# A Transformer-layer kernel on one core: second-half weight blocks of the MLP in a ring of tiles kept to the end, right operands of its last two products and the last rows' sums made among its middle products

## The chip, the core and the metric

The kernel runs on one core of one Trainium2 chip. The metric is the device time of one execution in microseconds (us); lower is better. Times of the program as a whole are given as the median of the runs, a profile is of one execution. TensorE is the matrix engine (PE in the rows), VectorE (DVE) and ScalarE (ACT) do the elementwise work, GpSimd (POOL) does a little, and SyncE (SP) issues the DMAs.

## The reference

One layer with a latent stream of 1024 tokens and 1024 channels, and a context of 256 tokens. All is float32. A mixer (adaLN, a projection, spatial gating, a two-way chunkwise mLSTM and an output projection) is followed by an MLP with 4096 hidden channels; each adds to the stream through a LayerNorm:

```python
def channel_mlp(h, w1, b1, w2, b2):
    return jnp.square(jax.nn.relu(h @ w1 + b1)) @ w2 + b2

def deepnorm_update(x, y, gate, g, b):
    return layer_norm(ALPHA * x + gate * y, g, b)

# in reference(), for the one layer:
y_l = mixer_output(u_l, v_l, hb_l, o_l, w_s[l], b_s[l], ln_v_g[l], ln_v_b[l], hn_g[l], w_out[l])
x_new = deepnorm_update(x, y_l, g1, ln1_g[l], ln1_b[l])
x_new = deepnorm_update(x_new, channel_mlp(modulate(x_new, sh2, sc2), w1[l], b1[l], w2[l], b2[l]),
                        g2, ln2_g[l], ln2_b[l])
```

## The kernel before

The mixer takes the time up to about 490 us; the MLP takes the rest. Each of the MLP's two matrix products is cut in two by two blocks and computed with seven block products in place of eight, so their operands are blocks, or sums and differences of blocks. A float32 operand is split into a high part (a cast on ScalarE) and a low part (a subtraction on VectorE), and each block product is three passes on TensorE: high by low, high by high, low by high (`mmk`, L983).

**Phase 1** (h times w1, then the squared ReLU) goes over 16 groups of 128 hidden channels per half, in batches of 4, 3, 3, 3 and 3 (`BATCHES`). For each group there are two weight blocks of 128x1024: X (`load_x`, L1075) and Y (`load_y`, L1079). `prep_w1(p, g)` makes the right operand wc_p_g of product p for group g: of X alone for p = 2 and 1, and for p = 5 the difference w1z of X and Y (kept for p = 7) and the sum of the two halves of Y (L1098, L1100), for p = 6 and 3 further differences of X (L1103, L1106), and then cast and low part (L1112, L1113). The left operands are h itself for p = 2 and 1, and sums of its parts for the others: `t_add` forms them (T2 for p = 6 stands in a tile of its own, L1149), `t_split` makes the parts T50h, T50l, T51h and so on (L1164, L1165). The first four groups are special: `first(2, g)` and `first(1, g)` (L1307) run while the last token tiles of h are still being made (`h2_half`), with casts of X made earlier (x0h, x0l). Then the loop over `steps` runs: for the first batch the products 5, 6, 3, 7 and 4, four groups each (12 matmuls of 128x512 a group), and then the other batches with all seven. Ahead of each step `prep_to` prepares operands LA = 5 steps ahead, `load_to` issues loads LD = 6 steps further ahead, and `tplan` says before which step which T sum and T part is made.

**Phase 2** (the hidden blocks times w2) goes over the products 1, 2, 6, 5, 3, 7, 4 and in each over 8 steps c. A step takes a block a of the left operand (loaded from DRAM, where phase 1 left it) and a right operand of w2 (`p2_load`, L1190), splits both (`p2_prep`, L1209: the parts of a go to pb, those of the right operand to wh and wl, L1206 and L1207), and multiplies for four token tiles (`p2_mm`, 24 matmuls). The right operands are T1 = b11, for p = 2 b21, for p = 6 T2 = b22 minus T1, for p = 5 T1 again (by then b12 minus b11), for p = 3 b22, for p = 7 b22 minus b12 (L1234), for p = 4 b21 minus T2 (L1239); for the last two, b12 and b21 are loaded once more as b12b and b21b in the steps of 7 and 4 themselves. The loop prepares LA2 = 3 steps ahead and asks for loads LD2 = 2 steps further ahead. After a product's last step the sums in PSUM are evacuated: after p = 3 c12 (L1471, L1472) and after p = 7 c22 (L1476, in a tile of the pool whose name shows as pm).

**The end.** The rows of the first four token tiles are finished among the steps of products 7 and 4 (`half1`, L1436). Of product 4 the steps c = 4 to 7 are done token tile by token tile, and each of the last four tiles t = 0 to 3 is finished behind its matmuls: residual (L1422), the gated sum r (L1488, L1491), `finish` (L1424) with the row sum (L1428), mean, variance (ScalarE), power (GpSimd) and the two steps of the last LayerNorm (L1430, L1431), and the output store. The last tile goes in two column halves of 256 and takes its statistics with BN_STATS (L1495 to L1511).

**Tiles and order.** Phase 1 and 2 share a ring of 38 slots of 4 KB per partition, `uslots`: `ualloc` takes the slot that has been free longest, `ufree` puts one back. 9 of the slots (ur) exist from before the first groups, 29 (ul) only when the mixer's pools (wpool, rawp and others) are closed behind `first(1, 3)`. rawp is a pool of four turning buffers for raw weight blocks of the mixer. Each engine runs its instructions in program order, with semaphores for what it needs of others; every DMA of the program is issued by SP, in program order too.

```python
    for g in range(3):
        load_x(g)
    ...
    rst.close()
    wst.close()
    u_open(ctx, USLOTS[1], "ul")
    ...
    for g in range(n0):
        load_y(g)
    load_x(3)
```

## Time and profile before

| what | value |
|---|---|
| median of three runs | 1126.34 us (1125.4 to 1127.55) |
| the profiled execution | 1127.33 us |
| its span, first to last instruction | 1125.4 us |
| busy share of the span: PE / PEld / DVE / ACT / POOL | 97% / 80% / 68% / 46% / 5% |
| DMA traffic | 208.08 MB, mean 185 GB/s |
| the chain of work that ended last, by engine | PE 89%, DVE 4%, DMA 3%, ACT 2% |

A span is the time between the first and the last instruction in the records; the execution's own time is 1.9 us longer. The granted clock of TensorE is given for a stretch as a share of its full 2.4 GHz; 1.00 is all of it, 0.50 is its lower level of 1.2 GHz, and what lies between is a stretch with both. A start time plus a duration can lie behind the start of the next row of the same engine, since instructions overlap a little.

### The profile page before, as it was taken

Reading aid. Unit: us, or ns where it says so; the run is one execution under the profiler, and the core shown is the slowest. Engines: PE = TensorE matmul, PEld = TensorE weight load, DVE = VectorE, ACT = ScalarE, POOL = GpSimd, SP = SyncE. Lnnn points to the kernel's source line nnn. Section 1 sums busy time; section 2 is a strip of 40 time slices with the busy share of each in tenths; the row PEclk is TensorE's granted clock in tenths of the full one; section 3 lists DMA queues with packets and bytes.
Section 4 is the critical chain, followed back from the end, with each engine's and each line's share of the span. In section 5 each row is a group of like instructions: output and inputs, shape, how many; then the busy total and the mean of one; then the engine's idle time right before and its main releaser. Section 6 shows DMA issues by size and latency. Waiting matters only on the chain.

```text
span 1125.4 us, 14624 instructions
## 1 busy us (share of the span) xinstructions
PE 1094.6 (97%) x5271; PEld 899.9 (80%) x5271; DVE 761.5 (68%) x1363; ACT 517.6 (46%) x821; POOL 53.6 (5%) x81
## 2 busy tenths in 40 slices
PE   8999999899999999997999999999999999999996
PEld 6899788777777888885888888888888888887875
DVE  4793666677775367659974747474667555468997
ACT  3585543321121236567755555556534334434341
POOL 0010000000101011110000000000000000001101
PEclk9999999999999999998999999999999999999999
DMA  8782579776453773233454435355997334356911
GB/s 319 259 280 95 169 255 293 236 204 175 127 155 113 260 238 129 85 112 112 151 195 127 175 123 183 112 197 201 321 413 271 113 90 152 96 168 235 326 57 75
DMA packets 92416, 208.08 MB, mean 185 GB/s; under 512 B 10037, under 2 KB 31413, under 8 KB 92089
## 3 DMA queue, kind: packets, MB, share of 16 engines
q1 hardware_dynamic: 92344, 207.16, 55.0%
q8 instruction: 41, 0.67, 0.2%
q14 instruction: 31, 0.25, 0.1%
HBM read 155.91 MB, written 51.21 MB: 184 GB/s over the span
## 4 chain that ended last, share of the span: by engine, by line
PE 89%; DVE 4%; DMA 3%; ACT 2%; issue 1%; POOL 1%; SPq 0%; DVEq 0%; ACTq 0%; POOLq 0%
PE A L986 29%; PE B L986 23%; PE wo L209 3%; PE wo L207 3%; PE wo L208 3%; PE n L736 2%; PE n L735 2%; PE pa L270 2%; PE v L207 2%; PE vg L209 1%; PE vg L208 1%; PE vg L207 1%; PE u L207 1%; PE v L209 1%; PE v L208 1%; PE u L209 1%
## 5 line engine op out<-in xcount | busy, mean ns | idle before, releaser
L986 PE MATMUL A<-wh,pb 128*128 128x512 f32 (+1 forms) x528 | 158.6, 383 | 0.0
L986 PE MATMUL B<-wh,pb 128*128 128x512 f32 x384 | 118.7, 390 | 0.0
L986 PEld LDWEIGHTS A<-wh,pb 128*128 128x128 f32 x528 | 98.0, 188 | 19.8
L986 PE MATMUL A<-wl,pb 128*128 128x512 f32 (+1 forms) x264 | 101.7, 385 | 3.2 <-DVE nmu_n L874 1.5
L986 PEld LDWEIGHTS B<-wh,pb 128*128 128x128 f32 x384 | 72.1, 188 | 15.6
L986 PE MATMUL B<-wl,pb 128*128 128x512 f32 x192 | 74.9, 390 | 0.0
L1206 ACT CAST pb<-a_S 128x1024 fp32r<-128x1024 f32 x32 | 33.7, 1053 | 75.1 <-PE B L986 43.8
L880 POOL TENSOR_TENSOR rs_n<-ve_n,mhalf 128x1 f32<-128x1 f32 x23 | 29.4, 1279 | 720.2 <-DVE ve_n L878 681.4
L1113 DVE TENSOR_TENSOR wc<-w1x,wc 128x512 fp32r<-128x512 f32 x56 | 38.3, 692 | 35.9 <-ACT wc L1112 35.9
L1207 DVE TENSOR_TENSOR wl<-b,wh 128x1024 fp32r<-128x1024 f32 x40 | 48.7, 1222 | 19.9 <-ACT wh L1206 6.9
L986 PEld LDWEIGHTS A<-wl,pb 128*128 128x128 f32 x264 | 49.6, 188 | 14.5 <-DVE nmu_n L874 1.7
L1207 DVE TENSOR_TENSOR pb<-a_S,pb 128x1024 fp32r<-128x1024 f32 x32 | 39.1, 1223 | 31.7 <-ACT pb L1206 31.5
L1206 ACT CAST wh<-b 128x1024 fp32r<-128x1024 f32 x40 | 42.0, 1051 | 33.4 <-DVE pb L1207 16.0
L207 PE MATMUL wo<-lo_W,yh 128*128 128x512 f32 x128 | 52.0, 406 | 0.0
L209 PE MATMUL wo<-hi_W,yl 128*128 128x512 f32 x128 | 50.7, 396 | 0.0
L208 PE MATMUL wo<-hi_W,yh 128*128 128x512 f32 x128 | 50.5, 394 | 0.0
L207 PE MATMUL vg<-lo_VG,Hhi 128*128 128x264 f32 x160 | 45.9, 287 | 0.0
L209 PE MATMUL vg<-hi_VG,Hlo 128*128 128x264 f32 x160 | 45.4, 284 | 0.5 <-DVE Hlo L198 0.5
L707 ACT ACTIVATE nmb<-nmb 128x512 f32<-128x512 f32 x16 | 10.1, 633 | 76.8 <-DVE nmb L706 46.6
L208 PE MATMUL vg<-hi_VG,Hhi 128*128 128x264 f32 x160 | 45.3, 284 | 0.0
L1112 ACT CAST wc<-w1x 128x512 fp32r<-128x512 f32 x56 | 34.4, 619 | 22.4 <-PE A L986 10.6
L1206 ACT CAST pb<-a_A 128x1024 fp32r<-128x1024 f32 x24 | 25.3, 1054 | 41.4 <-PE A L986 20.3
(412 smaller groups left out, 2773.7 us busy)
## 6 DMA issues: line engine op xcount, KB each, us to landing
ad<-in_wada SPq DMA_DIRECT2D x32, 512.0 KB, 6.1
b<-in_w SPq DMA_DIRECT2D x32, 512.0 KB, 5.2
a_S<-d_S SPq DMA_DIRECT2D x32, 512.0 KB, 4.1
d_S<-hF SPq DMA_DIRECT2D x50, 256.0 KB, 2.2
a_A<-d_A SPq DMA_DIRECT2D x24, 512.0 KB, 5.0
d_A<-hF SPq DMA_DIRECT2D x36, 256.0 KB, 2.0
wa<-in_wada SPq DMA_DIRECT2D x16, 512.0 KB, 6.2
w1x<-in_w SPq DMA_DIRECT2D x16, 512.0 KB, 3.6
```

What stands on the lines that cost most here:

```text
L207: T.matmul(o, ahi, blo, start=start, stop=False)
L208: T.matmul(o, ahi, bhi, start=False, stop=False)
L209: T.matmul(o, alo, bhi, start=False, stop=stop)
L270: T.matmul(pa[:, 0:256], s32[:, k, :], rv[k // 4][:, k % 4, :], start=(k == 0), stop=(k == KT - 1))
L735: T.matmul(pn[:, hh, :], nmb[d][:, h, :], vc[:, h, :], start=True, stop=False)
L736: T.matmul(pn[:, hh, :], wib[o : o + 64, h, :], st[o : o + 64, h, :], start=False, stop=True)
L880: G.tensor_tensor(rs, ve, mhalf[:, :1], op=ALU.pow)
L986: T.matmul(o, a, b, start=start and i == 0, stop=stop and i == 2, skip_group_check=more)
L1112: S.copy(t[:, 0:512], src)
L1113: V.tensor_tensor(t[:, 512:1024], src, t[:, 0:512].bitcast(F32), ALU.subtract)
L1206: S.copy(hi, src)
L1207: V.tensor_tensor(lo, src, hi.bitcast(F32), ALU.subtract)
```

## The change

**Loads of the first Y blocks.** rawp is opened ahead of wpool and kept to the end; its buffers become four named tiles raw0 to raw3, used in turn (`raw_tile`). Behind the casts of the first four X blocks, `load_y(0)` to `load_y(3)` load the Y blocks into these four tiles, and the tiles then stay in the ring as slots. The ring has 38 slots as before: 10 early ones (ur), 24 late ones (ul) and these four; `UL_ORDER` gives the order in which the late ones come into it. Two X blocks are loaded early now, where three were, and the other two behind the closing of the pools. `prep_w1(5, 0)` is called ahead of the last `h2_half`, and in the loop `load_to` and `prep_to` now stand ahead of the step's T sums and parts.

**Right operands of the last two products.** b12b is loaded in the steps of p = 3, and b22 minus b12 is formed in place there (L1252); b21b is loaded in the steps c < 4 of p = 3 and c >= 4 of p = 5, and T2 is replaced there by b21 minus T2 (L1256). The steps of p = 7 and p = 4 only split.

**Last rows.** `second(t)` takes, for each of the last four token tiles, the residual and the half of r that is complete after p = 7, with its row sum (L1444, L1445); the four are done one behind each of the steps c = 0 to 3 of p = 4. `finish` then sums only the other half (L1455) and adds the two sums (L1456). For the last tile the matmuls of both column halves come first, then all of VectorE's work on them.

```diff
@@ -29,8 +29,9 @@
...
 BATCHES = (4, 3, 3, 3, 3)
-USLOTS = (9, 29)
+USLOTS = (10, 24)
 SLOT = 2112
+UL_ORDER = (*range(15, 24), 0, *range(1, 15))
 ADA_SPLIT = 3
@@ -75,13 +76,19 @@
...
+    raw_n = [0]
+    def raw_tile(name):
+        raw_n[0] += 1
+        return rawp.tile([P, SLOT // 2], F32, tag=f"raw{(raw_n[0] - 1) % 4}", bufs=1, name=name)
...
         for i in range(2):
-            raw = rawp.tile([P, SLOT // 2], F32, tag="raw", name=f"raw_{name}_{i}")
+            raw = raw_tile(f"raw_{name}_{i}")
             dma(raw[:, :h], src[:, i * h : (i + 1) * h])
@@ -970,8 +977,7 @@
...
         pool = stack.enter_context(tc.tile_pool(name=name, bufs=1, reuse_waits="tile", **kw))
-        for i in range(n):
-            uslots.append((pool, f"{name}{i}"))
+        return [(pool, f"{name}{i}") for i in range(n)]
@@ -1076,8 +1082,8 @@
...
-    def load_y(g):
-        raws[g, "Y"] = ualloc(f"w1y_{g}")
+    def load_y(g, t=None):
+        raws[g, "Y"] = ualloc(f"w1y_{g}") if t is None else t
         dma(raws[g, "Y"][0], I["w1"][g, 1])
@@ -1197,10 +1203,10 @@
...
             keep["B22", c] = u_load(f"b22_{c}", I["w2"][1, 1, c])
-        elif p == 7:
-            p2w[p, c] = u_load(f"b12b_{c}", I["w2"][0, 1, c])
-        elif p == 4:
-            p2w[p, c] = u_load(f"b21b_{c}", I["w2"][1, 0, c])
+        elif p == 3:
+            p2w["12", c] = u_load(f"b12b_{c}", I["w2"][0, 1, c])
+        if p == (3 if c < 4 else 5):
+            p2w["21", c] = u_load(f"b21b_{c}", I["w2"][1, 0, c])
@@ -1230,19 +1236,24 @@
...
             src = free[-1][0]
-            free.append(p2w.pop((p, c)))
-            V.tensor_tensor(src, src, free[-1][0], ALU.subtract)
         else:
-            free.append(p2w.pop((p, c)))
+            free.append(keep.pop(("T2", c)))
             src = free[-1][0]
-            free.append(keep.pop(("T2", c)))
-            V.tensor_tensor(src, src, free[-1][0], ALU.subtract)
         wh, wl = ualloc(f"wh_{p}_{c}", F32R), ualloc(f"wl_{p}_{c}", F32R)
...
+        if p == 3:
+            free.append(p2w.pop(("12", c)))
+            t = keep["B22", c][0]
+            V.tensor_tensor(t, t, free[-1][0], ALU.subtract)
+        if p == (3 if c < 4 else 5):
+            free.append(p2w.pop(("21", c)))
+            t = keep["T2", c][0]
+            V.tensor_tensor(t, free[-1][0], t, ALU.subtract)
         for x in free:
@@ -1288,20 +1299,24 @@
...
     for g in range(n0):
-        raw = rawp.tile([P, SLOT // 2], F32, tag="raw", name=f"x0_{g}")[:, :1024]
+        raw = raw_tile(f"x0_{g}")[:, :1024]
         dma(raw, I["w1"][g, 0])
...
         wc[2, g], wc[1, g] = (pair((hi, lo), 0), None), (pair((hi, lo), 512), None)
+    for g in range(n0):
+        i = raw_n[0] % 4
+        load_y(g, (raw_tile(f"w1y_{g}")[:, :1024], (rawp, f"raw{i}")))
     p3r.close()
-    u_open(ctx, USLOTS[0], "ur", "right")
+    uslots += u_open(ctx, USLOTS[0], "ur", "right")
     for i in range(2):
...
             ctile[2 * i + h, "A11"] = t[:, h * 512 : h * 512 + 512]
-    for g in range(3):
+    for g in range(2):
         load_x(g)
@@ -1320,20 +1335,17 @@
...
     t_both(5, 1)
+    prep_w1(5, 0, (0, 0))
     h2_half(7, 1)
...
     early.close()
-    rst.close()
     wst.close()
-    u_open(ctx, USLOTS[1], "ul")
-    order = [17, 18, 19, 16, 1, *range(20, USLOTS[1]), 0, *range(2, 16)]
-    old = {t: (q, t) for q, t in uslots}
-    uslots[:] = [x for x in uslots if not x[1].startswith("ul")] + [old[f"ul{i}"] for i in order]
-    for g in range(n0):
-        load_y(g)
-    load_x(3)
+    ul = u_open(ctx, USLOTS[1], "ul")
+    uslots += [ul[i] for i in UL_ORDER]
+    for g in range(2, n0):
+        load_x(g)
     f = hF[0]
@@ -1345,7 +1357,7 @@
...
     LA, LD = 5, 6
-    prepped = nx
+    prepped = nx + 1
     loaded = {(p, g) for g in range(n0) for p in ("X", "Y")}
@@ -1384,11 +1396,10 @@
...
         p, g, b = steps[si]
-        prep_to(si + 1)
+        load_to(si + LA + LD)
+        prep_to(si + LA)
         for t in tplan.get(si - nx, []):
             t()
-        load_to(si + LA + LD)
-        prep_to(si + LA)
         p1_step(p, g, b == 0)
@@ -1421,11 +1432,28 @@
...
-    def finish(t, r, slot):
+    r2 = {}
+    def second(t):
+        tok = 4 + t
+        residual(tok)
+        r, slot = ualloc(f"r_{tok}")
+        hi = slice(512, 1024)
+        sm = mp_tile([P, 1], "sm3", 4, f"sm3_{t}")
+        V.tensor_tensor(r[:, hi], c22[t], g2l[:, hi], ALU.mult)
+        V.scalar_tensor_tensor(r[:, hi], r[:, hi], 1.0, xts[tok][0][:, hi], ALU.mult, ALU.add, accum_out=sm)
+        r2[t] = (r, slot, sm)
+    def finish(t, r, slot, sm1=None):
...
         sm = mp_tile([P, 1], "sm2", 2, f"sm2_{t}")
-        V.scalar_tensor_tensor(r, r, 1.0, x, ALU.mult, ALU.add, accum_out=sm)
+        if sm1 is None:
+            V.scalar_tensor_tensor(r, r, 1.0, x, ALU.mult, ALU.add, accum_out=sm)
+        else:
+            V.scalar_tensor_tensor(r[:, 0:512], r[:, 0:512], 1.0, x[:, 0:512], ALU.mult, ALU.add, accum_out=sm)
+            V.tensor_tensor(sm, sm, sm1, ALU.add)
         nmu, rs = stats_sum(mp, r, sm, x, f"n2_{t}")
@@ -1475,30 +1503,27 @@
...
                     load_xt(4 + t)
+                    todo.append(lambda t=t: second(t))
     for f in todo:
...
         tok = 4 + t
-        last = t == 3
-        r, slot = ualloc(f"r_{tok}")
-        residual(tok)
-        x = xts[tok][0]
-        if not last:
-            V.tensor_tensor(r[:, 512:1024], c22[t], g2l[:, 512:1024], ALU.mult)
+        r, slot, sm = r2[t]
+        if t < 3:
             for c in range(4, 8):
...
             V.tensor_tensor(r[:, 0:512], pA2[t], g2l[:, 0:512], ALU.mult)
-            finish(tok, r, slot)
+            finish(tok, r, slot, sm)
         else:
+            x = xts[tok][0]
             st6 = mp_tile([P, 3, 6], "st6", 1, "st6")
-            V.tensor_tensor(r[:, 512:1024], c22[t], g2l[:, 512:1024], ALU.mult)
-            V.tensor_tensor(r[:, 512:1024], r[:, 512:1024], x[:, 512:1024], ALU.add)
             V.bn_stats(st6[:, 0, :], r[:, 512:1024])
-            for i in range(2):
-                cs = slice(i * 256, (i + 1) * 256)
+            halves = [slice(i * 256, (i + 1) * 256) for i in range(2)]
+            for cs in halves:
                 for c in range(4, 8):
                     p2_mm(4, c, [t], cs)
+            for i, cs in enumerate(halves):
                 V.tensor_tensor(r[:, cs], pA2[t][:, cs], g2l[:, cs], ALU.mult)
...
```

How instructions move is shown at three places, first the names: a number behind a name is the group or step, and a trailing one counts tiles.

VectorE, before, from the T2 sums to the first operand of product 5 (w1z and w1y are the difference and the sum, wc_5_0 is the operand's low part):

```order
L1149 TENSOR_TENSOR T2_0_5104<-hF_4025 128x1024
L1149 TENSOR_TENSOR T2_1_5144<-hF_4025 128x1024
L1165 TENSOR_TENSOR T30l_5187<-hF_4025,T30h_5186 128x1024
L1098 TENSOR_TENSOR w1z_0_5098<-w1x_0_4905,w1y_0_5088 128x512
L1165 TENSOR_TENSOR T60l_5107<-T2_0_5104,T60h_5106 128x1024
L1100 TENSOR_TENSOR w1y_0_5088<-w1y_0_5088 128x512
L1098 TENSOR_TENSOR w1z_0_5098<-w1x_1_4907,w1y_1_5090 128x512
L1098 TENSOR_TENSOR w1z_2_5115<-w1x_2_4909,w1y_2_5092 128x512
L1113 TENSOR_TENSOR wc_5_0_5101<-w1y_0_5088,wc_5_0_5101 128x512
```

VectorE, after, first the piece among the last LayerNorm work of the mixer:

```order
L1104 TENSOR_TENSOR w1z_0_5061<-w1x_0_4913,w1y_0_4899 128x512
L916 SCALAR_TENSOR_TENSOR x1_7_4853,sm_7_4781<-r_7_4780,rs_n1_7_4860,ln1_3830 128x1024
L1106 TENSOR_TENSOR w1y_0_4899<-w1y_0_4899 128x512
L881 TENSOR_SCALAR nmu_n0_7_4866<-sm_7_4781 128x1
L1104 TENSOR_TENSOR w1z_0_5061<-w1x_1_4915,w1y_1_4901 128x512
L1109 TENSOR_TENSOR w1x_0_4913<-w1y_0_4899,w1x_0_4913 128x512
L1106 TENSOR_TENSOR w1y_1_4901<-w1y_1_4901 128x512
L885 TENSOR_SCALAR ve_n0_7_4870<-vs_n0_7_4868 128x1
L1112 TENSOR_TENSOR w1x_0_4913<-w1x_0_4913 128x512
L920 TENSOR_SCALAR z2_7_4865<-x1_7_4853,nmu_n0_7_4866,rs_n0_7_4872 128x1024
L1040 TENSOR_TENSOR c11_0_4911<-A_1_4980,c11_0_4911 128x512
L1119 TENSOR_TENSOR wc_5_0_5064<-w1y_0_4899,wc_5_0_5064 128x512
```

And behind that, the piece from the T50 parts to the low part of the third group's operand:

```order
L1171 TENSOR_TENSOR T50l_5053<-hF_4025,T50h_5052 128x1024
L1171 TENSOR_TENSOR T51l_5058<-hF_4025,T51h_5057 128x1024
L1040 TENSOR_TENSOR c11_1_4912<-A_3_5076,c11_1_4912 128x512
L1155 TENSOR_TENSOR T2_0_5123<-hF_4025 128x1024
L1119 TENSOR_TENSOR wc_5_1_5105<-w1y_1_4901,wc_5_1_5105 128x512
L1119 TENSOR_TENSOR wc_6_0_5120<-w1x_0_4913,wc_6_0_5120 128x512
L1104 TENSOR_TENSOR w1z_2_5108<-w1x_2_5099,w1y_2_4903 128x512
L1119 TENSOR_TENSOR wc_6_1_5144<-w1x_1_4915,wc_6_1_5144 128x512
L1106 TENSOR_TENSOR w1y_2_4903<-w1y_2_4903 128x512
L1104 TENSOR_TENSOR w1z_2_5108<-w1x_3_5101,w1y_3_4905 128x512
L1171 TENSOR_TENSOR T60l_5126<-T2_0_5123,T60h_5125 128x1024
L1119 TENSOR_TENSOR wc_5_2_5111<-w1y_2_4903,wc_5_2_5111 128x512
```

w1z_0, w1y_0 and the low part of wc_5_0 moved from behind T60l to ahead of the T50 parts; the preparation of group 2 stands between the T2 sum and T60l.

SP, before, the loads of the first blocks (d_x1 and d_A11 are stores):

```order
L43 DMA w1x_0_4905<-in_w1 128x1024
L43 DMA w1x_1_4907<-in_w1 128x1024
L43 DMA w1x_2_4909<-in_w1 128x1024
L43 DMA d_A11_0_121<-c11_0_4903 128x512
L43 DMA d_x1_116<-x1_7_4853 128x1024
L43 DMA d_A11_0_121<-c11_0_4903 128x512
L43 DMA d_A11_1_122<-c11_1_4904 128x512
L43 DMA w1y_0_5088<-in_w1 128x1024
L43 DMA w1y_1_5090<-in_w1 128x1024
```

SP, after, the same place:

```order
L44 DMA w1y_0_4899<-in_w1 128x1024
L44 DMA d_x1_116<-x1_6_4758 128x1024
L44 DMA w1y_1_4901<-in_w1 128x1024
L44 DMA w1y_2_4903<-in_w1 128x1024
L44 DMA w1y_3_4905<-in_w1 128x1024
L44 DMA w1x_0_4913<-in_w1 128x1024
L44 DMA w1x_1_4915<-in_w1 128x1024
L44 DMA d_A11_0_121<-c11_0_4911 128x512
L44 DMA d_x1_116<-x1_7_4853 128x1024
L44 DMA d_A11_0_121<-c11_0_4911 128x512
L44 DMA d_A11_1_122<-c11_1_4912 128x512
L44 DMA w1x_2_5099<-in_w1 128x1024
```

The four w1y loads moved ahead of the w1x loads and of the stores of A11; w1x_2 moved behind three of those stores.

VectorE, before, the end of product 7 (L1476 evacuates its four sums, L1239 forms b21 minus T2):

```order
L1207 TENSOR_TENSOR pb_7210<-a_A22_2_8943,pb_7210 128x1024
L1239 TENSOR_TENSOR b21b_2_8945<-b21b_2_8945,t2_2_7843 128x1024
L1476 TENSOR_TENSOR pm_7282<-A2_0_7297,pm_7282 128x512
L1476 TENSOR_TENSOR pm_7282<-A2_1_7298,pm_7282 128x512
L1207 TENSOR_TENSOR wl_4_2_9021<-b21b_2_8945,wh_4_2_9020 128x1024
L1476 TENSOR_TENSOR pm_7282<-A2_2_7299,pm_7282 128x512
L1476 TENSOR_TENSOR pm_7282<-A2_3_7300,pm_7282 128x512
L1207 TENSOR_TENSOR pb_7210<-a_A22_3_8978,pb_7210 128x1024
```

VectorE, after, the same place (L1504 is the evacuation, L1433 the residual of a last row tile):

```order
L1433 SCALAR_TENSOR_TENSOR xt_4_9059<-xt_4_9059,pm_7281 128x1024
L1433 SCALAR_TENSOR_TENSOR xt_5_9062<-xt_5_9062,pm_7281 128x1024
L1213 TENSOR_TENSOR wl_4_5_9149<-t2_5_7954,wh_4_5_9148 128x1024
L1213 TENSOR_TENSOR pb_7209<-a_A22_2_8962,pb_7209 128x1024
L1213 TENSOR_TENSOR wl_4_4_9112<-t2_4_7918,wh_4_4_9111 128x1024
L1504 TENSOR_TENSOR pm_7281<-A2_0_7296,pm_7281 128x512
L1504 TENSOR_TENSOR pm_7281<-A2_1_7297,pm_7281 128x512
L1504 TENSOR_TENSOR pm_7281<-A2_2_7298,pm_7281 128x512
L1504 TENSOR_TENSOR pm_7281<-A2_3_7299,pm_7281 128x512
L1213 TENSOR_TENSOR pb_7209<-a_A22_3_8994,pb_7209 128x1024
```

The subtractions are gone from here, residuals came in, and the evacuation's four parts stand together.

VectorE, before, near 202 us in the mixer (adacc is an adaLN sum over loaded blocks ad, kw an operand of the mLSTM's state product):

```order
L405 SCALAR_TENSOR_TENSOR adacc_181<-ad_25_2261,silu_cc_105,adacc_181 128x1024
L405 SCALAR_TENSOR_TENSOR adacc_181<-ad_26_2327,silu_cc_105,adacc_181 128x1024
L652 TENSOR_SCALAR og_2_0_2254<-og_2_0_2254,hng_500 128x512
L595 TENSOR_TENSOR kw_2_2271<-ptk_2_2268,cols_179 128x4x64 x2
L405 SCALAR_TENSOR_TENSOR adacc_181<-ad_27_2330,silu_cc_105,adacc_181 128x1024
```

VectorE, after, the same place:

```order
L602 TENSOR_TENSOR kw_2_2271<-ptk_2_2268,cols_179 128x4x64 x2
L659 TENSOR_SCALAR og_2_0_2254<-og_2_0_2254,hng_500 128x512
L412 SCALAR_TENSOR_TENSOR adacc_181<-ad_26_2327,silu_cc_105,adacc_181 128x1024
L620 SCALAR_TENSOR_TENSOR St5_1754<-St4_1753,carry_180,St5_1754 128x129 x4
L412 SCALAR_TENSOR_TENSOR adacc_181<-ad_27_2330,silu_cc_105,adacc_181 128x1024
```

kw_2 moved from behind the sum of block 26 to ahead of it.

## Rows read from the trace of the kernel before

**Rows 1.** Windows, products 5, 3, 7: stretch, length, busy (instructions), PEclk, DMA share, GB/s.

```profile
937.00:981.00 44.00, 44.00 (x195) 36.23 (x194) 21.52 (x18) 18.81 (x20) 0.00 (x0) 1.00 0.40 121
981.00:1025.00 44.00, 43.88 (x193) 35.86 (x192) 29.71 (x26) 16.73 (x20) 0.00 (x0) 1.00 0.54 179
1025.00:1070.00 45.00, 43.98 (x192) 35.95 (x192) 43.42 (x56) 19.75 (x24) 8.91 (x4) 1.00 0.85 300
```

**Rows 2.** TensorE's waits over the span: line, waited for, us in total, times, longest.

```profile
PE B L986 <- ACT wc L1112: 7.6, 1, 7.6
...
PE kv L605 <- issue: 2.2, 1, 2.2
...
PE A L986 <- DVE c L1472: 1.0, 1, 1.0
...
PE A L986 <- DVE pm L1476: 0.7, 2, 0.5
```

**Rows 3.** Windows around the start of product 5 in phase 1.

```profile
500.00:505.00 5.00, 5.00 (x26) 4.17 (x25) 0.68 (x2) 2.16 (x4) 0.00 (x0) 1.00 0.14 52
...
520.00:525.00 5.00, 5.00 (x17) 3.97 (x16) 5.00 (x9) 3.08 (x5) 0.00 (x0) 0.72 0.00 0
```

**Rows 4.** Timeline of TensorE, same place: start, us, instruction, [idle before <- releaser].

```profile
518.31 0.79 PE L986 MATMUL B<-T50l,wc 128*128 128x512 f32 x1 [7.57 <-ACT wc L1112]
...
523.39 0.40 PE L986 MATMUL B<-T50l,wc 128*128 128x512 f32 x1
```

**Rows 5.** Timeline of VectorE, same place.

```profile
511.78 2.35 DVE L1149 TENSOR_TENSOR T<-hF 128x1024 f32<-128x1024 f32 x2
...
515.18 0.69 DVE L1098 TENSOR_TENSOR w1z<-w1x,w1y 128x512 f32<-128x512 f32 x1
515.79 1.22 DVE L1165 TENSOR_TENSOR T60l<-T,T60h 128x1024 fp32r<-128x1024 f32 x1
516.92 0.69 DVE L1100 TENSOR_TENSOR w1y<-w1y 128x512 f32<-128x512 f32 x1
```

**Rows 6.** Timeline of ScalarE, same place.

```profile
517.64 0.62 ACT L1112 CAST wc<-w1y 128x512 fp32r<-128x512 f32 x1 [1.41 <-DVE w1y L1100]
```

**Rows 7.** Timeline of SP, DMA issues of the first weight blocks (start and length of the issues).

```profile
482.54 8.35 SPq L43 DMA_DIRECT2D w1x<-in_w  x3
...
507.10 3.78 SPq L43 DMA_DIRECT2D w1y<-in_w  x3
```

**Rows 8.** DMA issues of the page: count, KB each, median us to landing.

```profile
b<-in_w SPq DMA_DIRECT2D x32, 512.0 KB, 5.2
...
w1x<-in_w SPq DMA_DIRECT2D x16, 512.0 KB, 3.6
```

**Rows 9.** Line L1234: durations in ns (least/median/most), first and last start.

```profile
L1234 DVE TENSOR_TENSOR b<-b,b12b x8: 1215/1224/1226, 984.7 to 1047.2; 128x1024 f32<-128x1024 f32 x8
```

**Rows 10.** Timeline of VectorE in the tail.

```profile
1098.49 0.69 DVE L1491 TENSOR_TENSOR r<-A,pm 128x512 f32<-128x512 f32 x1
1099.21 1.23 DVE L1428 SCALAR_TENSOR_TENSOR r<-r,xt 128x1024 f32<-128x1024 f32 x1
...
1100.48 0.15 DVE L874 TENSOR_SCALAR nmu_n<-sm 128x1 f32<-128x1 f32 x1
...
1104.94 0.68 DVE L1491 TENSOR_TENSOR r<-A,pm 128x512 f32<-128x512 f32 x1
...
1118.04 0.42 DVE L1502 TENSOR_TENSOR r<-A,pm 128x256 f32<-128x256 f32 x1
...
1119.75 1.41 DVE L1510 SCALAR_TENSOR_TENSOR r<-r,mvf,pm 128x512 f32<-128x512 f32 x2
```

**Rows 11.** Timeline of VectorE near 202 us.

```profile
201.90 1.28 DVE L405 SCALAR_TENSOR_TENSOR adacc<-ad,silu_cc,adacc 128x1024 f32<-128x1024 f32 x1 [3.07 <-DMA ad<-in_wada]
...
203.50 0.75 DVE L595 TENSOR_TENSOR kw<-ptk,cols 128x256 f32<-128x256 f32 x2
```

**Rows 12.** Window behind it.

```profile
205.00:210.00 5.00, 5.00 (x19) 4.01 (x18) 3.47 (x7) 3.57 (x6) 0.00 (x0) 0.66 1.00 313
```

8 lines of the change are left out of this document (4 added, 4 removed).

## The prediction

> **What bounds the kernel now.** The windows by product first [rows 1]: through products 5 and 3 TensorE is busy for all of the time, VectorE for half to two thirds of it. So work that is only taken from another engine gives nothing there. What can be gained is the time in which TensorE stands, the time in which its clock is low, and the tail after its last product. The list of TensorE's waits names the stands [rows 2]: one of 7.6 us is longer than all the others together that this change can touch. It lies where the first right operand that is made of a difference of weight blocks, wc of product 5, is late. The windows show what follows it: 0.72 of the clock from 520 to 525 [rows 3], that is, part of this stretch at 1.2 GHz instead of 2.4. I price wait and clock together, from the rows of the matmuls [rows 4]: the first product-5 group starts at 518.31 after 7.57 us, so it could have started at 510.74; the second starts at 523.39. From 937 to 981 there are 195 matmuls in 44.00 us [rows 1], 0.226 us each; I take 0.229, a product's 192 in 44.0, for the few that a trace can miss. A group of 12 takes 2.75 us at that pace, and took 12.65 from the point where it could have begun: **9.9 us lost**, 7.6 by the wait and 2.3 by the clock.
>
> Why is the operand late? The VectorE rows [rows 5] show it: the T sums of both halves (511.78) and T60l stand before w1y (L1100, 516.92), and the cast at 517.64 waits for that [rows 6]. And the w1y loads were issued only at 507.10 [rows 7], because their tiles come from the pool that opens there.
>
> **The change part by part.** *Early loads and first preparation.* The w1y blocks go into tiles that exist already, and are issued behind the x0 casts, where three w1x loads were issued from 482.54 on [rows 7]; with 3.6 us from issue to landing [rows 8] all are there by some 495. Nine half-width VectorE operations of 0.6 us (the step from 515.18 to 515.79 [rows 5]), the whole preparation of product 5's group 0 and the sums of group 1, then run among the last LayerNorm work before 505; from 500 to 505 VectorE is busy for 0.68 us [rows 3]. Cover: these 5.4 us; without it they would delay the last h tile and so the start of product 5. What is late next is the third group, of w1x_2 and w1y_2: w1x_2 is issued only when the old pools are closed, where the first w1y was before, at 507.10, and lands near 511. VectorE's queue, from the T2 sum at 511.78 on: T2_0 1.17 (half of the 2.35 for two), six half-width operations at 0.60, T60l 1.13 (515.79 to 516.92), then the low half of the third operand, 0.69 until it is visible: 511.78 + 1.17 + 3.60 + 1.13 + 0.69 = 518.4. TensorE, started at 510.74, wants it at its third matmul of group three: 510.74 + 2 x 2.75 + 2 x 0.229 = 516.7. So **1.7 us stay** (bounds: 0, if two of the six operations find room before 511, and 4, if w1x_2 lands 2 us late, which VectorE cannot overtake). The fourth group and product 6 follow with 2 us of room or more by the same count. Gain 9.9 - 1.7 = **8.2** (5.9 to 9.9).
>
> *Sixteen subtractions of the last two products' right operands* (1.22 us each [rows 9]) leave the prepared steps of products 7 and 4. VectorE is busy there for 43.4 of 45 us [rows 1], and TensorE's waits 1.0 and 0.7 on VectorE's evacuations (L1472, L1476) [rows 2] come of that: those stand behind these subtractions. They now stand in products 5 and 3, where VectorE is busy for 21.5 and 29.7 of 44 us each; six of them are in the second already (the first at 984.7), so ten more make 51.2 + 12.2 = 63.4 of 88: hidden. Their 16 loads go the same way, and SP's queue now holds loads that wait for a slot which VectorE's subtraction frees. Behind them wait the a loads of the next steps; these are asked for two steps ahead, so a delay of one subtraction and one landing, 1.2 + 5.2 us [rows 8], stays under the 11 us of two steps. In products 7 and 4 six and eight operations go, but the second halves of the last four rows come in (four full-width residuals, four products, four sums, some 10 us), so VectorE stays near its limit: walking its order from 1025 on, I find both evacuations at or under 0.1 us of their need. Gain 1.7 - 0.1 = **1.6** (0 to 2.0).
>
> *The tail.* VectorE, not TensorE, sets it: a row tile takes 6.45 us (1098.49 to 1104.94 [rows 10]), TensorE's 24 matmuls for it 5.5. In each of three tiles the row sum shrinks from 1.23 us at full width to some 0.70 (half of the 1.41 for two half-width ones), and one tiny addition of 0.15 comes in: 3 x 0.38 = 1.1 saved; the third tile loses the three operations of the last tile's first half that were slipped in, 0.2. But these three now stand behind the third tile, on the path: operations of 0.42 that partly overlap, 0.8 to 1.3, taken as 1.0. The evacuated bank costs TensorE no wait any more, but it ends before VectorE either way. Gain **0.4** (0 to 0.8; the loss is excluded only down to -0.2).
>
> *The raw ring.* It keeps four tiles, but in another address range and with fixed turns, so some early loads change places on SP's queue. TensorE's 2.2 us [rows 2] near 202 (a kv product) is the place: kw (203.50) stands behind an adaLN sum whose load is late, 3.07 us of idle VectorE [rows 11], and the clock falls to 0.66 after it [rows 12]. In the new order kw stands ahead of that sum. But the next U load comes behind an output store, which waits for VectorE, and the next kv product then waits for it, by my walk 2.4 us. So most of the 3.4 (2.2 and some 1.2 of clock) only moves. Gain **0.5** (-2 to 3.4).
>
> Sum: 8.2 + 1.6 + 0.4 + 0.5 = 10.7. The profiled execution took 1127.33, its span 1125.4 and 1.9 around it; so 1116.6. It lies 1.0 above the median of the runs shown, 1126.34, and inside their spread, so against the median **1115.6**.
>
> **The rivals.** *The clock falls again.* After the 7.6 us the clock was low, after the 2.2 us too (0.66 in 205 to 210 [rows 12]); with waits of 1.0 and 0.7 in it, 1025 to 1070 shows 1.00 [rows 1]. My remaining 1.7 lies between. If it suffices, the 2.3 us of half clock stay: 1117.9. The Trainium skill ("TensorE: Matmul & The Clock Gate", section "HAM oscillation — how this bites in real kernels") says that waits between groups of matmuls send the array back to the low clock, and that this is paid again at each of them; by that rule this rival would be the forecast, and of the four rows two speak for it and two against.
>
> *VectorE is later than I count* (the w1x_2 load, or the last tile's LayerNorm pushed by the early operations): the third group 4 us late, 2.3 us of clock with it: 1115.6 + 2.3 + 2.3 = 1120.2. For it: VectorE works without a gap from 511.78 to 516.92 [rows 5], so what comes late stays late.
>
> *The early wait goes whole*, since the store in front of the U load is free sooner than I think: 1115.6 - 2.9 = 1112.7.
>
> *Evacuations stay late* in products 7 and 4, since VectorE is as full as before: 1117.2.
>
> *The order does not do it*: the loads come early, but their work stays behind the T sums. Then 8.2 is missing: 1123.8. The order speaks against it (w1y of the first group is fourteen rows ahead of T50l).
>
> *Slower.* In products 5 and 3 the loads take turns with the subtractions: each load waits for the slot that the subtraction before frees. Then a step takes 5.2 for the landing, 1.22 and 1.22 for the subtraction and the low half, 7.6 against 5.5 of TensorE; over 16 steps 34 us, less the lead of three prepared steps, 16.5: 17 us lost, 1132.6. It decides from the point where this loop is longer than a step. Against it: loads overlap, three were issued within 3.8 us [rows 7], and three slots or more are in turn.
>
> **How the numbers follow.** 0.2%, 2.3 us, is about what can be told from no change. Forecast 0.60, with its own range 1113.5 to 1117.5; clock 0.12; later VectorE 0.08; early wait gone 0.08; evacuations 0.05; order 0.02; slower 0.05. The time is the forecast's, 1115.6. The range, 1111.5 to 1119.5, takes in the early gain and the clock and leaves out the last two, most of the later VectorE and a little of each end. Faster: all but the last two, 0.92; the order's case lies at the edge of no change, 0.03; slower 0.05.
>
> **What would show it.** In the new profile: no wait of over 2 us of TensorE on a wc cast, one of 1 to 2 us near 517 on VectorE's low half of wc; 1.00 of the clock in the windows there; the waits on the c and pm evacuations gone; VectorE's tile period about 6.1 in the tail; near 202 no wait, but one near 210. Wrong, if TensorE shows waits in products 5 or 3, if the window behind 517 is below 1.00, or if the phase before 500 is longer than it was.

## The result, and the profile of the changed kernel

| | before | after |
|---|---|---|
| median of 8 runs, us | 1126.24 (1125.40 to 1129.29) | 1120.34 (1118.43 to 1123.11) |
| profiled execution, span, us | 1127.33, 1125.4 | 1122.52, 1120.5 |

The ratio is 0.9946 (95% interval 0.9931 to 0.9961): faster by 5.9 us, where 10.7 were forecast, and the median lies 0.8 above the range. The profiled execution lies 2.2 above the median of its kernel, which matters below.

TensorE's waits over the span of the changed kernel (line, waited for, us in total, times, longest) answer [rows 2]:

```profile
PE kv L612 <- DVE kw L602: 5.6, 4, 2.6
...
PE B L992 <- ACT hF L932: 1.2, 1, 1.2
PE A L992 <- DVE pm L1504: 0.6, 1, 0.6
```

The 7.6 us on wc and the 1.0 on c are gone; a wait of 1.2 stands at the same place in the program, for another reason. The waits on kw in the mixer have grown, from one of 1.0 to four of 5.6 us together. The windows (stretch, length, busy, PEclk, DMA share, GB/s) answer [rows 1, 3, 12]:

```profile
160.00:165.00 5.00, 3.90 (x15) 3.32 (x16) 2.27 (x7) 1.47 (x4) 0.00 (x0) 0.69 0.68 195
205.00:210.00 5.00, 5.00 (x28) 4.19 (x28) 2.54 (x5) 3.00 (x6) 0.00 (x0) 1.00 0.73 278
215.00:220.00 5.00, 2.94 (x11) 2.78 (x12) 4.28 (x6) 1.58 (x5) 0.00 (x0) 0.66 0.86 224
500.00:505.00 5.00, 5.00 (x25) 4.13 (x24) 4.75 (x10) 3.71 (x8) 0.17 (x1) 1.00 0.41 163
...
520.00:525.00 5.00, 4.98 (x22) 3.67 (x21) 5.00 (x8) 5.00 (x9) 0.00 (x0) 1.00 0.03 12
937.00:981.00 44.00, 44.00 (x195) 36.25 (x194) 33.10 (x29) 20.56 (x22) 0.00 (x0) 1.00 0.74 252
981.00:1025.00 44.00, 44.00 (x194) 36.15 (x194) 31.83 (x30) 18.35 (x20) 0.00 (x0) 1.00 0.49 156
```

VectorE works in 500 to 505 now (4.75 us, 0.68 before), the clock behind the start of product 5 is 1.00 (0.72 before), and products 5 and 3 carry the moved subtractions with TensorE still busy for all of the time. The low clock has moved: 1.00 at 205 to 210, but 0.69 and 0.66 at 160 and at 215.

Where the time went is seen when the same matmul is looked up in both traces and its start in the one is taken from that in the other. The changed kernel is 0.3 us early at 150, 4.3 late at 170, 4.2 late at 510, 4.1 early at 535, 2.8 early at 1000, 4.4 early at 1080. So the mixer lost 4.2, the start of product 5 gained 8.2, 1.2 were lost between 535 and 1000, where TensorE never waits, and 1.6 came back by 1080, at the evacuations ahead of product 7 and behind it. The 1.2 is small, but turned out to be the most useful number of the case.

### The profile page after: what moved, and what is told of

Its sections match the earlier page's. It is cut to its first block, busy times and chain, and to the rows that moved or that the text cites. A ratio compares the mean times of both kernels' runs of the same rounds, so it can differ in the third digit from the quotient of the medians.

```text
span 1120.5 us, 14642 instructions
## 1 busy us (share of the span) xinstructions
PE 1094.6 (98%) x5271; PEld 898.9 (80%) x5271; DVE 762.6 (68%) x1373; ACT 514.9 (46%) x821; POOL 53.9 (5%) x81
## 4 chain that ended last, share of the span: by engine, by line
PE 85%; DMA 6%; DVE 4%; ACT 2%; issue 1%; POOL 1%; SPq 0%; DVEq 0%; POOLq 0%; ACTq 0%
PE A L992 27%; PE B L992 23%; PE wo L216 3%; PE wo L214 3%; PE wo L215 3%; PE n L743 2%; PE n L742 2%; PE pa L277 2%; PE v L214 2%; PE vg L216 2%; PE vg L215 2%; PE vg L214 2%; PE u L214 1%; DMA ad<-in_wada 1%; PE v L216 1%; PE v L215 1%
## 5 line engine op out<-in xcount | busy, mean ns | idle before, releaser
L1213 DVE TENSOR_TENSOR pb<-a_A,pb 128x1024 fp32r<-128x1024 f32 x24 | 29.3, 1221 | 25.7 <-ACT pb L1212 25.6
```

Of the source, the lines that this page charges most:

```text
L1213: V.tensor_tensor(lo, src, hi.bitcast(F32), ALU.subtract)
```

## The experiments

Kernels are compared by their ratio to the kernel before, which ran beside each of them (one thousandth is 1.13 us).

### What the turns of the raw tiles cost

SP's issues in the changed kernel (start, length), around the last loads of the mixer's weights:

```profile
112.15 0.33 SPq L44 DMA_DIRECT2D ad<-in_wada  x1
...
129.53 0.34 SPq L44 DMA_DIRECT2D raw_O<-in_win  x1
...
130.43 0.38 SPq L44 DMA_DIRECT2D raw_O<-in_win  x1
...
134.15 0.41 SPq L44 DMA_DIRECT2D raw_O<-in_win  x1
```

and in the kernel before, where the same three went out from 112.79 on, two of them here:

```profile
112.79 0.33 SPq L43 DMA_DIRECT2D raw_O<-in_win  x1
...
120.30 0.34 SPq L43 DMA_DIRECT2D raw_O<-in_win  x1
```

With fixed turns each half must wait for one certain tile: the second half of O0 for that of the gate row, which is stored at 127.34, the halves of O1 for those of two adaLN loads, the first of them summed at 128.77; a tile that is free at 112 goes to an adaLN load. VectorE's rows 160 us into the changed kernel show the end of the chain: kw of chunk 8 stands behind V0's late low half and an adaLN sum.

```profile
157.96 1.22 DVE L97 TENSOR_TENSOR lo_V<-raw_V,hi_V 128x1024 fp32r<-128x1024 f32 x1
159.10 1.28 DVE L412 SCALAR_TENSOR_TENSOR adacc<-ad,silu_cc,adacc 128x1024 f32<-128x1024 f32 x1
160.29 0.75 DVE L602 TENSOR_TENSOR kw<-ptk,cols 128x256 f32<-128x256 f32 x2
```

Experiment e1 gives the tiles out as they come free:

```diff
-        return rawp.tile([P, SLOT // 2], F32, tag=f"raw{(raw_n[0] - 1) % 4}", bufs=1, name=name)
+        return rawp.tile([P, SLOT // 2], F32, tag="raw", bufs=4, name=name)
...
```

> The changed kernel, with the four raw tiles taken as they come free (one tag of four buffers, as before the change) instead of in fixed turns; the tiles still stay open for the early w1y blocks, and all else is as changed. Theory (fixed turns): the second half of O0 had to wait for the tile of an adaLN load that was free only at 129.5 (issued 130.43 instead of 112.79), O1 with it, so VectorE did three 1.2 us low halves later, kw of chunks 9 and 8 came late and the clock fell. Then those loads go back to about 113, 120 and 127, TensorE has no wait over 1 us between 145 and 165 and none of 2.6 near 217, the 2.2 us near 204 is back, TensorE reaches 500 us some 4.4 us sooner than in the changed kernel, and the time is 1120.3 - 4.4 = 1115.9 (1115 to 1118). Rival (the loss before 500 is not of the turns, or it is given back behind): within 1 us of 1120.3.

(The tile that O0 waits for is the gate row's, not an adaLN load's as it says there.) Measured: 1116.71 us, ratio 0.9925 (0.9912 to 0.9937), 2.1 thousandths or 2.4 us faster than the changed kernel's ratio (3.6 by the medians); the two intervals overlap a little, so the size is known to some 2 us only. VectorE now waits for TensorE at kw of chunk 8, not the other way round, and the window is at full clock; the wait near 204 is back with its low clock:

```profile
156.72 0.76 DVE L602 TENSOR_TENSOR kw<-ptk,cols 128x256 f32<-128x256 f32 x2 [2.04 <-PE ptk L598]
```

```profile
160.00:165.00 5.00, 5.00 (x33) 4.47 (x32) 0.69 (x4) 1.74 (x2) 0.00 (x0) 1.00 0.26 91
205.00:210.00 5.00, 5.00 (x21) 4.35 (x21) 3.36 (x7) 3.58 (x6) 0.00 (x0) 0.74 0.99 310
```

At 500 us this kernel is 0.7 early against before, the changed one 4.2 late: 4.9 us in the profiled executions, as the theory says, but only 2.4 in the ratios. The difference is spread. Six other profiles below (e2, e3, e4, e6, e9, e11) have the changed kernel's order in the mixer; at 500 they are 4.0, 3.2, 2.2, 0.1, -0.2 and 0.7 us late. Against e1's 0.7 early, the turns cost 0.5 to 4.9 us from one profile to the next, and the changed kernel's own profile shows their worst. Each is one execution of another kernel, so how far one kernel's executions differ is not shown.

### Load or preparation at the start of product 5

e2 keeps the early loads, but puts the preparation back behind the T sums:

```diff
-    prep_w1(5, 0, (0, 0))
...
-    prepped = nx + 1
+    prepped = nx
...
-        load_to(si + LA + LD)
-        prep_to(si + LA)
+        prep_to(si + 1)
         for t in tplan.get(si - nx, []):
             t()
+        load_to(si + LA + LD)
+        prep_to(si + LA)
```

> The changed kernel, with the w1y blocks still loaded early, but with the preparation of product 5's right operands back behind the T sums (no early preparation of group 0, and the step's own preparation ahead of the T sums, the look-ahead behind them, as before). Theory (load and order are both needed): VectorE reaches w1y of group 0 only after both T sums and w1z, about 515.8, one 1.1 us operation sooner than before the change, so TensorE still waits some 6 us there with a low clock behind it: 1120.3 + 6.5 = 1126.8 (1125 to 1128). Rival (the late load alone was the cause): within 1 us of 1120.3, with a wait of 1 to 2 us at product 5.

Measured: 1126.02, ratio 0.9998 (0.9989 to 1.0008); all of the change's gain is gone. The wait, and the clock behind it:

```profile
PE B L992 <- ACT wc L1118: 4.2, 1, 4.2
```

```profile
515.00:520.00 5.00, 1.16 (x3) 0.51 (x3) 5.00 (x9) 4.74 (x7) 0.00 (x0) 0.72 0.14 52
520.00:525.00 5.00, 5.00 (x15) 3.95 (x15) 5.00 (x8) 1.75 (x3) 0.00 (x0) 0.59 0.00 0
```

So early loads alone shorten the wait from 7.6 to 4.2 (not to 6, as I had it), and leave the low clock.

e9 was to make the loads late and keep the order. The call of `load_y` stands where the old pools close, and group 0's early preparation goes:

```diff
-    for g in range(n0):
-        i = raw_n[0] % 4
-        load_y(g, (raw_tile(f"w1y_{g}")[:, :1024], (rawp, f"raw{i}")))
...
-    prep_w1(5, 0, (0, 0))
...
-    prepped = nx + 1
+    prepped = nx
...
     ul = u_open(ctx, USLOTS[1], "ul")
     uslots += [ul[i] for i in UL_ORDER]
+    for g in range(n0):
+        i = raw_n[0] % 4
+        load_y(g, (raw_tile(f"w1y_{g}")[:, :1024], (rawp, f"raw{i}")))
```

> The changed kernel with the w1y loads issued where the old pools close (about 507), into the same ring tiles; the preparation of a step stays ahead of the T sums in the loop, only that of group 0 among the first groups goes, since its block is not there yet. Together with e2_order this parts load and order. Theory (both are needed): w1y lands at about 511, so w1z and w1y of group 0 are 1 to 2 us ahead of where they were before the change, with the T sums pushed behind them: TensorE waits 4 to 6 us at product 5, 1120.3 + 5.5 = 1125.8 (1123.5 to 1127.5). Rival (the order alone would do): within 1.5 us of 1120.3.

Measured: 1124.97, ratio 0.9997 (0.9988 to 1.0005). It did not do what it was meant to: its tiles were free early, and the loads went out at 480.75, though their call stands behind the closing of the pools:

```profile
480.75 0.33 SPq L44 DMA_DIRECT2D w1y<-in_w  x1
483.75 5.79 SPq L44 DMA_DIRECT2D w1y<-in_w  x3
```

It says something else instead. With early loads and the loop's preparation ahead of the T sums, but without the early preparation of group 0, the wait is 4.2 us again. So the order in the loop does nothing for the first group; the early preparation takes the last 3 us. e11 makes the loads late by giving the blocks tiles of the pool that opens late:

```diff
...
-    uslots += [ul[i] for i in UL_ORDER]
+    uslots[:0] = [ul[i] for i in UL_ORDER]
+    for g in range(n0):
+        load_y(g)
     for g in range(2, n0):
         load_x(g)
+    uslots.extend((rawp, f"raw{i}") for i in range(4))
...
```

> In e9_late_y the w1y loads still went out at 480.75, since their tiles were free then; so load and order are not parted yet. This is the changed kernel with the w1y blocks in tiles of the left pool, which opens only when the old pools are closed, and with the preparation ahead of the T sums kept in the loop (group 0's early preparation goes, as in e9). Its tiles fall so that 1236 matmuls have different rests modulo 256, 118 more than in the changed kernel, 0.7 us. Theory (of the 7.6 us wait before the change the late load is worth some 3.4, since e2_order and e9_late_y, with early loads, both wait 4.2): the loads go out behind 505, TensorE waits about 7.6 us on the first wc of product 5, 1125.0 + 3.4 + 0.7 = 1129.1 (1127 to 1131). Rival (the load was never late enough to matter, only the place of the preparation): a wait of 4.2 us and 1125.7.

Measured: 1129.08, ratio 1.0034 (1.0021 to 1.0048), slower than before the change; the theory's 1129.1. The loads and the wait:

```profile
507.75 3.78 SPq L44 DMA_DIRECT2D w1y<-in_w  x3
```

```profile
PE B L992 <- ACT wc L1118: 7.0, 1, 7.0
```

The waits on this wc form a ladder: 7.0 with late loads, 4.2 with early loads, none with early loads and an early first preparation.

### The smaller terms

e3 puts the sixteen subtractions and their loads back into products 7 and 4:

```diff
-        elif p == 3:
-            p2w["12", c] = u_load(f"b12b_{c}", I["w2"][0, 1, c])
-        if p == (3 if c < 4 else 5):
-            p2w["21", c] = u_load(f"b21b_{c}", I["w2"][1, 0, c])
+        elif p == 7:
+            p2w[p, c] = u_load(f"b12b_{c}", I["w2"][0, 1, c])
+        elif p == 4:
+            p2w[p, c] = u_load(f"b21b_{c}", I["w2"][1, 0, c])
...
```

> The changed kernel, with the sixteen subtractions and their loads back in the preparation of products 7 and 4. Theory (prediction's second term): the waits of TensorE on the c and pm evacuations (1.0 and 0.7 in total before the change) come back, up to 1120.3 + 1.6 = 1121.9. Rival (the row sums that were moved in fill VectorE in products 7 and 4, so that with the subtractions back it falls behind by more than before): slower by 3 us or more. Second rival: the waits do not come back, within 0.5 us of 1120.3.

Measured: 1120.75, ratio 0.9961 (0.9949 to 0.9974), 1.7 us slower by the ratios, inside their intervals. The waits are back, though smaller than before the change:

```profile
PE A L992 <- DVE pm L1499: 0.6, 2, 0.4
PE A L992 <- DVE c L1495: 0.6, 1, 0.6
```

From start to start of the matmuls around them, before the change loses 2.2 us there, the changed kernel 0.8, e3 1.7. So the term is 1.4, for 1.6 forecast; 0.6 on pm stays.

e4 has the tail of before (full-width residual, product and sum per row tile, and the last tile's first half slipped in):

```diff
-                    todo.append(lambda t=t: second(t))
...
-            finish(tok, r, slot, sm)
+            finish(tok, r, slot)
```

> The changed kernel, with the tail as before: no second-half sums among product 4, full-width row sums in the tail, and the last tile's first half's sums slipped in before the third tile's scaling. Theory (prediction's third term): VectorE's period in the tail goes back from 6.1 to 6.45, and the time to 1120.3 + 0.4 = 1120.7 (1120.2 to 1121.2). Rival (the whole of the row sums, 1.1, is gained, since the last tile's own operations would have stood there anyway): 1121.4 or more.

Measured: 1119.72, ratio 0.9953 (0.9940 to 0.9967): 0.8 by the ratios, too little for them to tell. The rows tell it. VectorE's first operation of each row tile in e4, 6.44 apart, as in [rows 10]:

```profile
1091.38 0.69 DVE L1519 TENSOR_TENSOR r<-A,pm 128x512 f32<-128x512 f32 x1 [3.40 <-PE A L992]
...
1097.82 0.68 DVE L1519 TENSOR_TENSOR r<-A,pm 128x512 f32<-128x512 f32 x1
```

and in the changed kernel, 6.12 apart:

```profile
1094.07 0.69 DVE L1516 TENSOR_TENSOR r<-A,pm 128x512 f32<-128x512 f32 x1 [3.37 <-PE A L992]
...
1100.19 0.68 DVE L1516 TENSOR_TENSOR r<-A,pm 128x512 f32<-128x512 f32 x1
```

From that first operation to the end of the span it is 26.9 us in before and e4 and 26.4 in the changed kernel: 0.5 gained, the forecast's 0.4.

### Two paces of the same matmul

Back to the 1.2 us that the changed kernel loses from 535 to 1000. TensorE waits for nothing there, VectorE is busy for 1 us more of the 165 from 535 to 700 than before, DMA no more, and the clock is 1.00. But TensorE gets through fewer matmuls. Before:

```profile
535.00:700.00 165.00, 165.00 (x724) 135.69 (x723) 112.61 (x174) 99.73 (x162) 0.00 (x0) 1.00 0.48 163
```

After:

```profile
535.00:700.00 165.00, 165.00 (x721) 135.01 (x720) 113.60 (x175) 99.48 (x163) 0.00 (x0) 1.00 0.47 163
```

From start to start a matmul of 512 columns takes 0.2267 us, or more, 0.229 to 0.241. Before, 198 of 722 steps in this stretch are of the slower kind (0.229 us and up), after, 326 of 719, and which ones they are goes by tile: of the 72 that read the T50 and T51 parts, 68 are slow before and 70 after. I took the tiles' addresses from the two programs and sorted the steps from 535 to 1000 by whether the addresses of the moving operand (the left one, streamed through the array) and the stationary operand (the right one, held in it) have the same rest when divided by 256 bytes:

| | rests differ: slow of all | rests equal: slow of all |
|---|---|---|
| before | 411 of 464 | 119 of 1573 |
| after | 560 of 628 | 165 of 1403 |

The steps with different rests take 0.2325 us on average. All but two of the slow steps with equal rests have one with different rests among the twelve before or behind them. No pair of rests differs by anything but 0 or 128 bytes, and it is the difference that counts, not one operand's place: after, 374 of 424 are slow with 0 for the moving and 128 for the stationary operand, 186 of 204 the other way round, and 1 of 486 with 128 for both and no unequal pair within twelve. The change raised the number of matmuls with different rests in the whole program from 958 to 1118. Most of both are the tiles at the right end of SBUF, which had the other rest all along. The added ones come of the ring: a raw tile is 4224 bytes, 128 more than a multiple of 256, and two of the four now hold operands at the other rest (with the right-hand tiles moved by 128 bytes alone, 162 would be left). Two kernels test it. e5 makes all rests equal:

```diff
-    rpad.tile([P, 120], F32, name="rpad_t")
+    rpad.tile([P, 88], F32, name="rpad_t")
...
-        return rawp.tile([P, SLOT // 2], F32, tag=f"raw{(raw_n[0] - 1) % 4}", bufs=1, name=name)
+        return rawp.tile([P, SLOT // 2 + 32], F32, tag=f"raw{(raw_n[0] - 1) % 4}", bufs=1, name=name)
```

e6, the control, moves the right-hand tiles by 256 bytes, so that the rests stay:

```diff
-    rpad.tile([P, 120], F32, name="rpad_t")
+    rpad.tile([P, 56], F32, name="rpad_t")
```

> The changed kernel with two address changes only: the pad tile at the right end of SBUF is 88 instead of 120 floats (all right-hand tiles move by 128 bytes), and a raw tile is 32 floats wider (128 bytes, so all four lie at the same rest). It comes of this: from 535 to 1000 us TensorE waits nowhere, and still the changed kernel lost 1.2 us there, since more of its matmuls of 512 columns start 0.2333 us apart instead of 0.2267. In the program's addresses 560 of 628 with moving and stationary operand at different rests modulo 256 bytes are slow, of the 1567 at equal rests 165. Over the whole program 1118 of the changed kernel's fp32r matmuls of 512 columns are at different rests (958 before the change); this kernel has none. Theory (the pitch follows the rests): 1118 x 0.9 x 0.0066 = 6.6 us less, 1120.3 - 6.6 = 1113.7 (1112.5 to 1115), and under 20% slow pitches from 535 to 1000. Rival (the pitch follows what the other engines do, or on which side of SBUF a tile lies): within 1 us of 1120.3, half of the pitches from 535 to 700 still slow.

> Control for the address theory: the changed kernel with the pad at 56 instead of 120 floats, so that all right-hand tiles move by 256 bytes and the rests modulo 256 stay as they are (1118 matmuls at different rests, as in the changed kernel). Theory: no change, 1120.3 (1119 to 1121.5), 342 of the 719 pitches from 535 to 700 slow, as now. Rival (a shift of any size changes the pitches): the count of slow pitches from 535 to 700 differs by over 50.

(In the first, 1567 is a wrong total, the table's 1403 is right, and 0.2333 is too high for the mean of the slow steps, 0.2325; the 342 in both is 326 by the limit of 0.229 us.) Measured: e5 1111.19, ratio 0.9876 (0.9862 to 0.9889), 7.9 us faster than the changed kernel's ratio; e6 1118.48, ratio 0.9939 (0.9925 to 0.9953), the same within the intervals. From 535 to 700 e5 has no slow step, e6 326 of 719. From 535 to 1000 e5 gains 2.9 us on the kernel before, and e6 loses 1.1, as the changed kernel does. The windows of e5 and of e6:

```profile
535.00:700.00 165.00, 165.00 (x730) 136.62 (x729) 112.58 (x175) 102.23 (x167) 0.00 (x0) 1.00 0.46 160
```

```profile
535.00:700.00 165.00, 165.00 (x720) 135.03 (x720) 111.62 (x173) 100.55 (x164) 0.00 (x0) 1.00 0.46 161
```

A group of twelve with T50 and T51 as the changed kernel has it (first row to second row, 2.79 us):

```profile
588.00 0.40 PE L992 MATMUL B<-T50l,wc 128*128 128x512 f32 x1
...
590.79 0.40 PE L992 MATMUL B<-T50l,wc 128*128 128x512 f32 x1
```

and in e5 (2.72 us):

```profile
582.53 0.39 PE L992 MATMUL B<-T50l,wc 128*128 128x512 f32 x1
...
585.25 0.39 PE L992 MATMUL B<-T50l,wc 128*128 128x512 f32 x1
```

e10 sets the pad to 88 in the kernel before, and changes nothing else:

> The kernel before the change with one number changed: the pad at the right end of SBUF is 88 instead of 120 floats. In its program 958 fp32r matmuls of 512 columns have operands at different rests modulo 256 bytes; with this pad none has. Theory (e5_residue): 958 x 0.0066 x 0.9 = 5.7 us less than before the change, 1125.6 - 5.7 = 1119.9 (1118.5 to 1121), no slow pitch from 535 to 1000, and the waits at 204 and at product 5 as before. Rival (the gain of e5_residue came with the changed order, for instance from waits that a shorter mixer removes): within 1.5 us of 1125.6.

Measured: 1119.53, ratio 0.9946 (0.9932 to 0.9959). The 7.6 us wait is still there, no step from 535 to 700 is slow, and from 535 to 1000 it gains 3.2 us:

```profile
PE B L986 <- ACT wc L1112: 7.6, 1, 7.6
```

```profile
535.00:700.00 165.00, 165.00 (x730) 136.62 (x729) 111.41 (x173) 99.53 (x162) 0.00 (x0) 1.00 0.47 162
```

One number in the kernel before is worth as much as the whole change.

### A version that beats both

e7 is e1 with two calls exchanged in the loop over the o units:

```diff
-        ada2_steps(2)
         if seq:
             kv_do(1 if i < 6 else len(seq))
+        ada2_steps(2)
```

> The kernel of e1_turns, with the two adaLN steps behind the kv chunk in the loop that makes the o units, not ahead of it; so kw of chunk 2 stands ahead of the second adaLN sum whose load is late near 202. Theory (the wait near 204 is that sum's load and no other): the 2.8 us wait of TensorE and the low clock behind it go, 1116.7 - 4.0 = 1112.7. Rival (the wait moves to the next chunk, as in the changed kernel at 217): between 1115.5 and 1117.5, with a wait of 2 us or more near 211 to 220.

Measured: 1114.83, ratio 0.9907 (0.9894 to 0.9921), 2.0 us faster than e1 by intervals that overlap, half of the expected 4.0. The wait of 2.8 near 204 is down to 0.4, but two stand behind it, so each theory had half of it:

```profile
202.29 1.13 PE L612 MATMUL kv<-vac,kw 128*128 128x129 f32 x8 [0.44 <-issue]
210.80 1.13 PE L612 MATMUL kv<-vac,kw 128*128 128x129 f32 x8 [0.72 <-DMA ad<-in_wada]
217.95 1.13 PE L612 MATMUL kv<-vac,kw 128*128 128x129 f32 x8 [1.21 <-DVE kw L602]
```

e8 adds the two address changes of e5 to e7.

> All of it together: free raw tiles as they come, kv chunk ahead of the adaLN steps, and the two address changes. If each works alone and they add: 1120.3 - 3.6 - 4.0 - 6.6 = 1106.1; if the wait near 204 only moves: 1110.1; if the address theory is wrong: 1112.7 or more.

Measured: 1108.15, ratio 0.9844 (0.9830 to 0.9857), 17.5 us faster than before the change; the address changes add 7.1 to e7, so they add up with the rest. e12 is e8 with the first U weight prepared after the last o unit (`if i == 7` in place of `if i == 5`):

> The kernel of e8_all, with the first U weight prepared after the last o unit instead of after the sixth. In e8_all TensorE waits 1.8 us near 217 on kw, which stands behind U's low half on VectorE, and that behind U's load; here two adaLN sums stand there instead. Theory: this wait goes or falls under 0.5, and little is late next (U is first used behind the v units): 1108.2 - 1.8 = 1106.4. Rival (the adaLN loads take the same time, so kw waits for them instead): within 1 us of 1108.2.

Measured: 1108.21, ratio 0.9844 (0.9831 to 0.9858), nothing. The rival was right: the wait on kw falls to 0.3, and TensorE waits as long for an adaLN load:

```profile
PE kv L612 <- DMA ad<-in_wada: 1.6, 1, 1.6
...
PE kv L612 <- DVE kw L602: 0.3, 1, 0.3
```

## Why the prediction was wrong, and where it was right

| term | forecast | measured, in the profiled executions |
|---|---|---|
| start of product 5 | 8.2 | 8.2 |
| subtractions of products 7 and 4 | 1.6 | 1.4 |
| tail | 0.4 | 0.5 |
| raw ring, mixer | 0.5 | -4.2 |
| pace of the matmuls, 535 to 1000 | no term | -1.2 |
| sum | 10.7 | 4.7 (the spans differ by 4.9) |

*The early loads and the first preparation* are right in mechanism, and the loads and the preparation are both needed (e2, e9, e11). That the size is right to the tenth is luck: I had the remaining wait at the third group, 1.7 us on VectorE's low half. It stands at the first, 1.2 us on ScalarE's copy of the last h tile:

```profile
516.10 0.50 PE L992 MATMUL B<-T50l,wc 128*128 128x512 f32 x1 [1.18 <-ACT hF L932]
```

Before the change that copy ended within the 7.6 us and held up nothing, but its row was there to be read: it ends at 511.42, so product 5 could not have started at 510.74, and of the 9.9 us some 0.7 were not to be had.

```profile
509.91 1.51 ACT L925 ACTIVATE hF<-pth,mod 128x128 f32<-128x128 f32 x4
```

The third group's low half was there at 522.98 and TensorE used it at 523.23. Two things helped: three matmuls of product 6 stand ahead of that use in TensorE's order (from 522.43 on), and the nine half-width operations did run among the LayerNorm work and shortly behind it, three of their rows here:

```profile
500.25 0.69 DVE L1104 TENSOR_TENSOR w1z<-w1x,w1y 128x512 f32<-128x512 f32 x1 [1.57 <-DMA w1x<-in_w]
...
502.07 0.69 DVE L1106 TENSOR_TENSOR w1y<-w1y 128x512 f32<-128x512 f32 x1
...
503.33 0.68 DVE L1109 TENSOR_TENSOR w1x<-w1y,w1x 128x512 f32<-128x512 f32 x1
```

*The rival of the clock* (it falls again at product 5) did not come: 1.00 behind the 1.2 us wait. What I cited from the Trainium skill ("TensorE: Matmul & The Clock Gate", section "HAM oscillation — how this bites in real kernels"), that waits between groups of matmuls send the array back to the low clock, is shown there for waits of 3 to 5 us. The trace agrees for the 4.2 us of e2 (0.72 and 0.59); for waits as short as the 1.7 that I had left, the section decides nothing, so I was wrong to make this rival the forecast by that rule. The rival of the slow loop in products 5 and 3 did not come either.

*The raw ring* is the step that failed. I wrote that "some early loads change places on SP's queue", then priced one place, the one where the trace of before shows a wait. The places to look at were those where a load had moved back, and three had each moved behind the release of one certain tile, by 7 to 18 us; VectorE's work there was hidden before only because it came early. e1 shows that the turns cost 2.4 us in the ratios, and 4.9 in the profiled execution, where I had 0.5 of gain and 2 of loss as the bound. The place that I did price came out about as forecast: my walk at 217 was right (2.4 forecast, 2.6 measured, 1.4 to 2.3 in the other profiles of this order), and from 195 to 230 the changed kernel gains and loses nothing, where I had 0.5. The loss lies ahead of it: from 150 to 170 the changed kernel loses 4.6 us, e1 0.6. The prediction's own sign of an error, a longer phase before 500, is the one that came.

*The pace of the matmuls* had no term at all. I said of the ring that it lies "in another address range", and took that for nothing. e5, e6 and e10 show what it is worth: 1.2 of loss from 535 to 1000, and 6 to 8 to be gained by anyone who had asked.

*Small slips.* The parts of the tail's term (1.1, 0.2 and -1.0) add up to 0.3, not 0.4, and the chances of the five cases called faster to 0.93, not 0.92.

The medians add up within their spread: with e1's mixer (0.7 gained) less the 2.4 of the turns, 8.2 + 1.4 + 0.5 - 1.2 - 1.7 is 7.2, measured 5.9 (4.4 to 7.8 by the interval).

## What to carry to other kernels

When a change gives buffers fixed turns, list every load that moves back in its queue and the work that waits for it, not only the places that hurt before; a place without a wait may be one with hidden work. When TensorE loses time where it waits for nothing, count its matmuls per window before and after, and look at where their operands lie. Do this on the tuned kernel too: here one pad was worth as much as a rewrite.
